# Holding the low part of q on all 128 rows in the attention heads of a two-layer trunk

## The chip, the cores and the metric

The kernel runs on one core of one Trainium2 chip, as a single launch. The metric is the device time of that launch in microseconds, the median of several runs. The profile is of one execution and gives for each instruction its engine, its start and its duration. TensorE is called PE, its weight loads PEld, VectorE DVE, ScalarE ACT, GpSimd POOL and SyncE SP.

## What is computed

Two layers work on x of 256 tokens by 1024 features in float32. Each layer is a half-weight SwiGLU network, a mixer and a second SwiGLU network, each followed by a residual sum and a layer norm. Both mixers hold attention heads of width 64: layer 0 has 12 heads whose softmax is masked by a dilated pattern, layer 1 has 8 heads of stick-breaking attention beside 4 mLSTM heads of width 128. For a head, what matters here is only the product of q and k ahead of the softmax:

```python
scores = jnp.einsum("bdhnqe,bdhnke->bdhnqk", qb, kb).astype(jnp.float32) / math.sqrt(dh)   # layer 0
z = jnp.einsum("bhqd,bhkd->bhqk", qblk, kt).astype(jnp.float32) / math.sqrt(dh)            # layer 1
```

## The kernel before

**Split products.** Products run in the type float32r. Every operand is split into a high part, rounded to that type, and a low part, what is left; a product of two matrices is then high x high, high x low and low x high. Weights stream in 166 chunks of 1 MB (class `Weights`): SP loads a chunk into a raw buffer, ACT makes the high part (L83), DVE the low part (L84), in four pieces per chunk. The layer's activations lie transposed in `xh` and `xl`, and a projection (`mmB`, L211 to L218) runs, for half a chunk, 8 k-tiles x 3 products of 256 columns.

**The mixers.** `mixer0` (L559) and `mixer1` (L631) project q and k in groups of four heads: `proj_qk` (L550) takes two chunks, one with the q and one with the k of two pairs of heads. There are five groups, three in layer 0 and two in layer 1. A projection leaves two banks of 128 rows; rows 0 to 63 belong to the first head of a pair and rows 64 to 127 to the second. `HALF` names these two slices, `i` is the head in the pair and `j` the pair.

**The stacked layout.** Heads are 64 wide, the array has 128 rows. `stack_q` writes the high part of q on both halves of the rows for each head (`qq`, four copies on ACT, L460) and the low part only on the head's own half (`ql`, DVE, L462). `stack_k` writes the high part of k on the head's own half and its low part on the other half (`kk`, ACT L468, DVE L470). So one product of 128 rows, `qq` x `kk` (L477), sums high x high and high x low, and a second product of 64 rows, `ql` x the high half of `kk` (L478), adds low x high. `scores64` does this for two token tiles, so a head has four products on PE, taken in turn from L477 and L478.

**The order around them.** `steps()` is called after each half chunk of a projection and runs, for head k, the scores and the softmax (s1), for head k-2 the product with v (s3, L514, whose results take 64 columns of the array) and for head k-1 the transposes of its weights (s2, L483 on PE, then the copy L486 on ACT). The softmax is L581 to L588 in layer 0 and L703 to L714 in layer 1, on DVE and ACT. Its small memsets (L709, L710) run on POOL, as do the `pow` of every layer norm (L291) and a mask that layer 1's mixer builds (L638). The Tile framework plans the order of each engine's queue at compile time, by its own model of times, with data dependencies and buffer releases as its limits; `hp()` moves a block forward in it.

**Buffers.** `qq`, `ql` and `kk` come from the pool `gp`, tag "g": 11 slots, each of the size of the largest tile of the tag, 4 KB per row. The hidden tiles of the SwiGLU networks use the same slots.

Of the kernel before, what the change touches and what calls it, by code (L numbers as in the profile page):

```python
# [11 lines left out]
F32 = mybir.dt.float32  # L12
# [5 lines left out]
P = 128  # L18
# [10 lines left out]


class Weights:
    """Streams the weight matrices through SBUF in chunks of [128, 2048]: each
    is loaded once and split exactly into hi + lo, both float32r."""

    def __init__(self, nc, raw_pool, w_pool, chunks):
        self.nc, self.raw_pool, self.w_pool, self.chunks = nc, raw_pool, w_pool, chunks
# [9 lines left out]
        self.next = 0  # L46

    def load_part(self, j0, j1):
        """The first chunk, by quarters."""
        (ap,), k, c = self.chunks[0]  # L50
        if j0 == 0:
            self.raw[0] = self.raw_pool.tile([P, k * c], F32, tag="raw", name="raw0")
        rv = self.raw[0].rearrange("p (k c) -> p k c", k=k)
        for j in range(j0, j1):
            self.nc.sync.dma_start(rv[:, 2 * j:2 * j + 2, :], ap[:, 2 * j:2 * j + 2, :])
        self.loaded = 1
# [62 lines left out]
def kernel(ctx: ExitStack, tc: tile.TileContext, a, cmask, out):  # L119
# [34 lines left out]
    def MM():  # L154
        return ps_mm.tile([P, 512], F32, tag="mm", name=nm("mm"))

# [1 line left out]
    def cols(w, c0):  # L158
        return ([a[w][:, c0:c0 + 256].rearrange("(k p) c -> p k c", p=P)], 8, 256)

# [20 lines left out]
    chunks += ffn_chunks("l1_ffn2")  # L181
    W = Weights(nc, raw_pool, w_pool, chunks)

# [1 line left out]
    X = [const.tile([P, D], F32, name=f"X{t}") for t in range(2)]  # L185
    for h in range(2):
        for t in range(2):
# [19 lines left out]
        bcast(gb[:, 0, :], pre + "_g", D, nc.sync)  # L207
        bcast(gb[:, 1, :], pre + "_b", D, nc.sync)

# [1 line left out]
    def mmB(i, j, bank, off):  # L211
        hi, lo = W.get(i)
        cs = slice(j * P, (j + 1) * P)
# [44 lines left out]
        nc.scalar.copy(hi, src)  # L258
        nc.vector.tensor_tensor(lo, src, hi.bitcast(F32), OP.subtract)

# [1 line left out]
    def transpose_x(t, halves=(0, 1), scale=True):  # L262
        for hf in halves:
            b = MM()
# [32 lines left out]
                    nc.sync.dma_start(out[0, t * P:(t + 1) * P, hs], X[t][:, hs])  # L297

    def ln_last(t, accs):
        """The closing norm, by column groups in the order in which they end."""  # L300
        st = sm(24, "stl")
        mv = sm(4, "mvl")
        for c, w in COLS3:
            nc.vector.tensor_tensor(X[t][:, c:c + w], accs[c][:, 0:w], X[t][:, c:c + w], OP.add)
            for q in range(c // 256, (c + w) // 256):
                nc.vector.bn_stats(st[:, q * 6:q * 6 + 6], X[t][:, q * 256:(q + 1) * 256])
        nc.vector.bn_aggr(mv[:, 0:2], st)
        nc.vector.tensor_scalar(mv[:, 2:3], mv[:, 1:2], EPS, None, op0=OP.add)
        nc.gpsimd.tensor_tensor(mv[:, 3:4], mv[:, 2:3], mhalf[:, 0:1], OP.pow)
        for h in range(2):  # L310
            hs = slice(h * 512, (h + 1) * 512)
            nc.vector.scalar_tensor_tensor(Y[:, hs], X[t][:, hs], mv[:, 0:1], gb[:, 0, hs], OP.subtract, OP.mult)
        for q in range(4):
            qs = slice(q * 256, (q + 1) * 256)
            nc.vector.scalar_tensor_tensor(X[t][:, qs], Y[:, qs], mv[:, 3:4], gb[:, 1, qs], OP.mult, OP.add)
            (nc.sync, nc.scalar)[q % 2].dma_start(out[0, t * P:(t + 1) * P, qs], X[t][:, qs])

    def out_proj(ys, nxt, last=False, hooks=()):
        """Rows of ys (slots of two k-tiles) times the next chunks, residual and
        norm; the token tiles run one after the other over the last chunks, so  # L320
        that one's norm hides under the other's products. nxt: the stage that
        follows; hooks: run ahead of the first token tile's last chunks."""
        n = len(ys)
        ids = W.take(n)
        hooks = list(hooks)
        accs = [{c: ACC() for c, _ in COLS}, {}]
        cols = [COLS, COLS3 if last else COLS]

        def open_t1():
            for c, _ in cols[1]:  # L330
                accs[1][c] = MM() if c == 768 else ACC()

        if n > 4:
            open_t1()
        for c in range(n - 4):
            for t in range(2):
                mmO(ids[c], ys[c], t, accs[t], c == 0, False, cols[t])
                if t == 1:
                    W.free(ids[c])
                W.pump()  # L340
        for c in range(n - 4, n):
            h = hooks.pop(0) if hooks else None
            if h:
                h()
            mmO(ids[c], ys[c], 0, accs[0], c == 0, c == n - 1)
            W.pump()
        if n == 4:
            open_t1()
        ln_a(0, accs[0], last)
        if last:  # L350
            for g in COLS3:
                for c in range(n - 4, n):
                    mmO(ids[c], ys[c], 1, accs[1], False, c == n - 1, [g])
            ln_last(1, accs[1])
            return
        for c in range(n - 4, n):
            if c == n - 1:
                transpose_x(0)
            mmO(ids[c], ys[c], 1, accs[1], c == 0, c == n - 1)
            W.free(ids[c])  # L360
            W.pump()
        ln_a(1, accs[1])
        nxt()

    def stagger(n, per, done):
        """n chunks by token tiles, per of them to a bank: done(t, b, bank)."""
        ids = W.take(n)
        banks = {}
        for t in range(2):
            for c in range(n):  # L370
                if t == 0 and c == n - 1:
                    transpose_x(1)
                if c % per == 0:
                    banks[t] = MM()
                mmA(ids[c], t, banks[t], (c % per) * 256)
                if t == 1:
                    W.free(ids[c])
                W.pump()
                if c % per == per - 1:
                    done(t, c // per, banks[t])  # L380

# [1 line left out]
    def swiglu(bank):  # L383
        sg = T(256)
        nc.scalar.activation(sg, bank[:, 0:256], AF.Silu)  # L385
# [55 lines left out]
                split(y[:, j, 0, :], y[:, j, 1, :], g)  # L441
        out_proj(ys, nxt, last)

# [1 line left out]
    # scores of a head: [t1 s0 | t1 s1 | t0 s0], by (token tile, column, width)  # L445
    BLK = ((1, 0, 2 * P), (0, 2 * P, P))

    def scores(bank, q, k):
# [3 lines left out]
    HALF = (slice(0, 64), slice(64, 128))  # L452

    def stack_q(b, qq, ql):
        """q of two pairs of heads: hi over both halves of the rows for each
        head of a pair, lo where it stands."""
        v = b.rearrange("p (j t) -> p j t", j=2)
        for i, r in enumerate(HALF):
            for o in HALF[i:] + HALF[:i]:
                nc.scalar.copy(qq[o, i], v[r])  # L460
        for i, r in enumerate(HALF):
            nc.vector.tensor_tensor(ql[r], v[r], qq[r, i].bitcast(F32), OP.subtract)  # L462

    def stack_k(b, kk):
        """k likewise: hi where it stands, lo on the other half of the rows."""
        v = b.rearrange("p (j t) -> p j t", j=2)
        for i, r in enumerate(HALF):
            nc.scalar.copy(kk[r, i], v[r])  # L468
        for i, r in enumerate(HALF):
            nc.vector.tensor_tensor(kk[HALF[1 - i], i], v[r], kk[r, i].bitcast(F32), OP.subtract)  # L470

    def scores64(bank, qk, i, j):
        qq, ql, kk = qk
        r = HALF[i]
        for t, o, _ in BLK:
            ts = slice(t * P, (t + 1) * P)
            nc.tensor.matmul(bank[:, o:o + 256], qq[:, i, j, ts], kk[:, i, j, :], start=True, stop=False)  # L477
            nc.tensor.matmul(bank[:, o:o + 256], ql[r, j, ts], kk[r, i, j, :], start=False, stop=True)  # L478

    def transpose_p(p):  # L480
        b = MM()
# [41 lines left out]
    pair = []  # L523

    def slots():
        """y slots of two k-tiles, taken as they are first written."""
        got = {}

        def get(i):
            if i not in got:  # L530
                got[i] = GR()
            return got[i]

        return get

    def projB(dst, off, steps):
        """Two feature tiles of the next chunk into dst columns off.. (fp32)."""
        (i,) = W.take(1)
        b = MM()
        for j in range(2):  # L540
# [8 lines left out]

    def proj_qk(lst, steps):  # L550
        qq = g_pool.tile([P, 2, 2, S], F32R, tag="g", name=nm("qq"))
        ql = g_pool.tile([P, 2, S], F32R, tag="g", name=nm("ql"))
        stack_q(projB(None, 0, steps), qq, ql)
        kk = g_pool.tile([P, 2, 2, S], F32R, tag="g", name=nm("kk"))
        stack_k(projB(None, 0, steps), kk)
        lst.append((qq, ql, kk))

# [1 line left out]
    def mixer0():  # L559
        cw = sm(6, "cw")  # L560
        for c in range(2):
# [65 lines left out]
        assert step[0] == 12  # L627
        return [(yts, i) for i in (1, 2, 0, 3)], [steps, steps, conv_out]

# [1 line left out]
    def mixer1():  # L631
        gbias = sm(8, "gbias")
        bcast(gbias[:, 0:4], "l1_mlstm_b_i", 4)
        bcast(gbias[:, 4:8], "l1_mlstm_b_f", 4)
        bcast(msk[:, 384:896], "l1_mlstm_norm_g", 512)
        # strictly causal mask over [t1 s0 | t1 s1 | t0 s0]
        m3 = msk[:, 0:384]
        nc.gpsimd.memset(m3, 0.0)  # L638
        for o in (128, 256):
# [56 lines left out]
            nc.vector.tensor_copy(Bc, b[:, 0:8])  # L696
            nc.vector.tensor_tensor(ccv, gv[:, :, 0:4], Bc.rearrange("p (t c) -> p t c", t=2), OP.subtract)

        # stick-breaking heads
        def soft_sb(b):  # L700
            with hp():
                z = T()
# [14 lines left out]
        qs, qm = [], []  # L717
        sb = [att_head(qs, lambda t: vs[:, t * 512:(t + 1) * 512], h, yts, 4, soft_sb) for h in range(8)]

        # mLSTM heads  # L720
        nmu = sm(8, "nmu")
        den = sm(8, "den")
        num = []
# [72 lines left out]
        qkproj(qm)  # L796
        so = G()
        ids = W.take(2)
        # so: by pair of heads, token tile and head
        def final(g):  # L800
            def pv(tl):
                return tl.rearrange("p (t h) -> p t h", t=2)[:, :, 2 * g:2 * g + 2]
# [53 lines left out]
        final(1)  # L856
        return [(yts, i) for i in (2, 3, 0, 1)], [None, lambda: final_tr(0), None, lambda: final_tr(1)]

# [1 line left out]
    def start(banks):  # L860
        with tc.manual_schedule():
            for h in range(2):
# [35 lines left out]


def _pattern_mask():  # L900
    """8 ln(number of dilation patterns that pair t with s) over the blocks
    [t1 s0 | t1 s1 | t0 s0]; a shape-only constant."""
    i = np.arange(P)
    m = np.full((P, 3, P), 8 * NEG, np.float32)
    for b, (t0, s0) in enumerate(((P, 0), (P, P), (0, 0))):
# [26 lines left out]
```

## Time and profile before

| what | value |
|---|---|
| median of 3 runs | 1016.66 us (1014.95 to 1017.03) |
| span of the profiled execution | 1014.5 us |
| PE busy | 998.9 us (98%) |
| PE weight loads busy | 934.1 us (92%) |
| DVE busy | 617.7 us (61%) |
| ACT busy | 538.0 us (53%) |
| POOL busy | 20.9 us (2%) |
| read from HBM | 181.90 MB, 180 GB/s over the span |

The heads of layer 0 run from 236.8 to about 290 us, those of layer 1 from 729.6 to about 765 us. Busy times overlap between engines. The records of PE overlap too, because a matmul's end lies well behind the start of the next, so steps from start to start tell more of PE's pace than durations do.

### The profile page before, as it was taken

What the parts mean: (1) busy time and instruction counts of PE and PEld (TensorE: products, weight loads), DVE (VectorE), ACT (ScalarE), POOL (GpSimd) and SP (SyncE); (2) the same over time, 40 slices, a digit from 0 to 9 for tenths busy, and PEclk for the clock granted to TensorE, in tenths of its full rate; (3) what the DMA queues carried; (4) which work ended last, traced back from release to release, by engine and by line L of the source; (5) the groups of instructions that cost most, each with busy time, mean ns of one, the idle gap of its engine ahead of it and who ended that gap; (6) DMA issues with size and microseconds to landing.
All of it is one profiled execution on the core that took longest, in us unless ns stands there. A gap on an engine that the chain in (4) does not pass through costs nothing.

```text
span 1014.5 us, 17718 instructions
## 1 busy us (share of the span) xinstructions
PE 998.9 (98%) x7204; PEld 934.1 (92%) x7204; DVE 617.7 (61%) x1238; ACT 538.0 (53%) x1096; POOL 20.9 (2%) x54
## 2 busy tenths in 40 slices
PE   7999999999999999999999999999999999999997
PEld 6999998899879999998899999889989899999986
DVE  4765554667658756554675556447786786656434
ACT  4755453558646645443455555436776476545430
POOL 2000000000000000000000000000000100000000
PEclk9999999999999999999999999999999999999999
DMA  9876555474325755555476555646734367555511
GB/s 293 280 240 202 173 201 188 144 249 153 127 95 184 233 183 192 181 193 198 134 241 203 180 195 180 197 136 208 235 103 144 102 208 232 185 191 183 186 64 41
DMA packets 137314, 184.09 MB, mean 181 GB/s; under 512 B 4256, under 2 KB 121504, under 8 KB 137232
## 3 DMA queue, kind: packets, MB, share of 16 engines
q1 hardware_dynamic: 136672, 182.24, 54.5%
q8 instruction: 56, 0.92, 0.4%
q0 software_dynamic: 272, 0.47, 0.2%
q10 hardware_dynamic: 288, 0.26, 0.1%
q14 instruction: 26, 0.21, 0.1%
HBM read 181.90 MB, written 1.05 MB: 180 GB/s over the span
## 4 chain that ended last, share of the span: by engine, by line
PE 95%; DMA 2%; DVE 2%; ACT 1%; issue 0%; SPq 0%; POOL 0%; DVEq 0%; ACTq 0%; POOLq 0%
PE mm L218 17%; PE mm L216 17%; PE mm L217 17%; PE acc L251 9%; PE acc L253 9%; PE acc L255 9%; PE mm L236 4%; PE mm L235 4%; PE mm L237 4%; DMA raw<-in_l_ffn_w_in_dram 2%; PE acc L478 1%; PE acc L477 1%; PE mm L483 1%; PE mm L267 1%; PE acc L514 1%; DVE lo L84 1%
## 5 line engine op out<-in xcount | busy, mean ns | idle before, releaser
L84 DVE TENSOR_TENSOR lo<-raw,hi 128x512 fp32r<-128x512 f32 (+1 forms) x664 | 425.6, 685 | 254.0 <-ACT hi L83 252.8
L83 ACT CAST hi<-raw 128x512 fp32r<-128x512 f32 (+1 forms) x664 | 373.4, 618 | 295.8 <-PE mm L217 161.0
L216 PE MATMUL mm<-xh,hi 128*128 128x256 f32 x1456 | 411.2, 282 | 0.0
L218 PE MATMUL mm<-xh,lo 128*128 128x256 f32 x1456 | 409.4, 281 | 0.2 <-DVE lo L84 0.2
L217 PE MATMUL mm<-xl,hi 128*128 128x256 f32 x1456 | 409.0, 281 | 0.0
L218 PEld LDWEIGHTS mm<-xh,lo 128*128 128x128 f32 x1456 | 274.3, 188 | 0.7 <-DVE lo L84 0.4
L216 PEld LDWEIGHTS mm<-xh,hi 128*128 128x128 f32 x1456 | 274.4, 188 | 0.4
L217 PEld LDWEIGHTS mm<-xl,hi 128*128 128x128 f32 x1456 | 274.4, 188 | 0.0
L251 PE MATMUL acc<-hi,gr 128*128 128x512 f32 (+1 forms) x416 | 128.7, 387 | 0.0
L253 PE MATMUL acc<-lo,gr 128*128 128x512 f32 (+1 forms) x416 | 127.2, 384 | 0.0
L255 PE MATMUL acc<-hi,gr 128*128 128x512 f32 (+1 forms) x416 | 127.1, 384 | 0.0
L235 PE MATMUL mm<-hi,xh 128*128 128x256 f32 (+1 forms) x352 | 99.3, 282 | 0.0
L236 PE MATMUL mm<-lo,xh 128*128 128x256 f32 (+1 forms) x352 | 98.4, 279 | 0.0
L237 PE MATMUL mm<-hi,xl 128*128 128x256 f32 (+1 forms) x352 | 98.3, 279 | 0.0
L253 PEld LDWEIGHTS acc<-lo,gr 128*128 128x128 f32 x416 | 77.2, 188 | 15.1
L255 PEld LDWEIGHTS acc<-hi,gr 128*128 128x128 f32 x416 | 77.2, 188 | 14.9
L251 PEld LDWEIGHTS acc<-hi,gr 128*128 128x128 f32 x416 | 76.0, 188 | 14.6 <-issue 0.6
L236 PEld LDWEIGHTS mm<-lo,xh 128*128 128x128 f32 x352 | 66.2, 188 | 0.2
L235 PEld LDWEIGHTS mm<-hi,xh 128*128 128x128 f32 x352 | 66.2, 188 | 0.2
L237 PEld LDWEIGHTS mm<-hi,xl 128*128 128x128 f32 x352 | 66.2, 188 | 0.0
L385 ACT ACTIVATE t<-mm 128x256 f32<-128x256 f32 x88 | 33.6, 382 | 35.8 <-PE mm L218 27.8
L387 DVE SCALAR_TENSOR_TENSOR t<-t,mm 128x256 f32<-128x256 f32 x88 | 36.7, 417 | 13.1 <-ACT t L385 12.7
(163 smaller groups left out, 572.7 us busy)
## 6 DMA issues: line engine op xcount, KB each, us to landing
raw<-in_l_ffn_w_in_dram SPq DMA_DIRECT2D x87, 1024.0 KB, 5.1
raw<-in_l_ffn_w_out_dram SPq DMA_DIRECT2D x44, 1024.0 KB, 5.0
raw<-in_l_mix_w_in_dram SPq DMA_DIRECT2D x26, 1024.0 KB, 5.4
raw<-in_l_mix_w_out_dram SPq DMA_DIRECT2D x8, 1024.0 KB, 4.9
gb<-in_l_ln_g_dram SPq DMA_DIRECT2D x6, 512.0 KB, 5.4
gb<-in_l_ln_b_dram SPq DMA_DIRECT2D x6, 512.0 KB, 4.6
X<-in_x_dram SPq DMA_DIRECT2D x4, 256.0 KB, 4.9
raw<-in_l_ffn_w_in_dram SPq DMA_DIRECT2D x4, 256.0 KB, 8.5
```

The lines of the kernel that those rows point to most:

```text
L83: self.nc.scalar.copy(hi[:, sl], r[:, sl])
L84: self.nc.vector.tensor_tensor(lo[:, sl], r[:, sl], hi[:, sl].bitcast(F32), OP.subtract)
L216: nc.tensor.matmul(o, hi[:, kt, cs], xh[:, kt, :], start=kt == 0, stop=False)
L217: nc.tensor.matmul(o, hi[:, kt, cs], xl[:, kt, :], start=False, stop=False)
L218: nc.tensor.matmul(o, lo[:, kt, cs], xh[:, kt, :], start=False, stop=kt == 7)
L235: nc.tensor.matmul(o, xh[:, kt, ts], hi[:, kt, :], start=kt == 0, stop=False)
L236: nc.tensor.matmul(o, xh[:, kt, ts], lo[:, kt, :], start=False, stop=False)
L237: nc.tensor.matmul(o, xl[:, kt, ts], hi[:, kt, :], start=False, stop=kt == 7)
L251: nc.tensor.matmul(accs[c][:, 0:w], yh, hi[:, k, c:c + w], start=st, stop=False)
L253: nc.tensor.matmul(accs[c][:, 0:w], yh, lo[:, k, c:c + w], start=False, stop=False)
L255: nc.tensor.matmul(accs[c][:, 0:w], yl, hi[:, k, c:c + w], start=False, stop=sp)
L387: nc.vector.scalar_tensor_tensor(g, sg, 0.5, bank[:, 256:512], OP.mult, OP.mult)
```

## The change

`ql` gets a second index, the head in the pair, as `qq` has it, and is 128 rows for each head: the head's own half holds the low part of q and the other half zero. POOL writes the zeros, two memsets of 64 rows by 512 elements for each group. DVE writes the low parts as before, to their new place. In `scores64` the second product takes all 128 rows of `ql` and of `kk`; the rows of `kk` that hold the low part of k meet zeros. Comments and docstrings are dropped beside this, which does not alter the program.

```diff
@@ stack_q
         v = b.rearrange("p (j t) -> p j t", j=2)
+        for i, r in enumerate(HALF):
+            nc.gpsimd.memset(ql[HALF[1 - i], i].bitcast(F32), 0.0)
         for i, r in enumerate(HALF):
             for o in HALF[i:] + HALF[:i]:
                 nc.scalar.copy(qq[o, i], v[r])
         for i, r in enumerate(HALF):
-            nc.vector.tensor_tensor(ql[r], v[r], qq[r, i].bitcast(F32), OP.subtract)
+            nc.vector.tensor_tensor(ql[r, i], v[r], qq[r, i].bitcast(F32), OP.subtract)
@@ scores64
         qq, ql, kk = qk
-        r = HALF[i]
         for t, o, _ in BLK:
             ts = slice(t * P, (t + 1) * P)
             nc.tensor.matmul(bank[:, o:o + 256], qq[:, i, j, ts], kk[:, i, j, :], start=True, stop=False)
-            nc.tensor.matmul(bank[:, o:o + 256], ql[r, j, ts], kk[r, i, j, :], start=False, stop=True)
+            nc.tensor.matmul(bank[:, o:o + 256], ql[:, i, j, ts], kk[:, i, j, :], start=False, stop=True)
@@ proj_qk
-        ql = g_pool.tile([P, 2, S], F32R, tag="g", name=nm("ql"))
+        ql = g_pool.tile([P, 2, 2, S], F32R, tag="g", name=nm("ql"))
```

## Rows read from the trace of the kernel before

**Rows 1.** Page, part 4: the chain that ended last, by engine
```profile
PE 95%; DMA 2%; DVE 2%; ACT 1%; issue 0%; SPq 0%; POOL 0%; DVEq 0%; ACTq 0%; POOLq 0%
```
**Rows 2.** Timeline of PE, 234.8 to 238.3: start us, duration us, engine, line, tiles, rows
```profile
234.89 0.28 PE L218 MATMUL mm<-xh,lo 128*128 128x256 f32 x1
...
236.67 0.28 PE L218 MATMUL mm<-xh,lo 128*128 128x256 f32 x1
236.79 0.28 PE L477 MATMUL acc<-kk,qq 128*128 128x256 f32 x1
237.00 0.38 PE L478 MATMUL acc<-kk,ql 64*128 64x256 f32 x1
237.31 0.38 PE L477 MATMUL acc<-kk,qq 128*128 128x256 f32 x1
...
238.16 0.28 PE L217 MATMUL mm<-xl,hi 128*128 128x256 f32 x1
```
**Rows 3.** Timeline of PE's weight loads, same stretch and columns
```profile
236.67 0.19 PEld L477 LDWEIGHTS acc<-kk,qq 128*128 128x128 f32 x1
...
237.31 0.19 PEld L477 LDWEIGHTS acc<-kk,qq 128*128 128x128 f32 x1
```
**Rows 4.** Timeline of PE where L514 follows scores, and a projection (x8: merged)
```profile
249.67 0.28 PE L477 MATMUL acc<-kk,qq 128*128 128x256 f32 x1
...
250.81 0.87 PE L514 MATMUL acc<-t,g 128*64 128x256 f32 x8
...
743.62 0.27 PE L218 MATMUL mm<-xh,lo 128*128 128x256 f32 x1
743.82 0.87 PE L514 MATMUL acc<-t,g 128*64 128x256 f32 x8
```
**Rows 5.** Timeline of PE where the transposes follow a projection
```profile
246.38 0.28 PE L218 MATMUL mm<-xh,lo 128*128 128x256 f32 x1
246.50 0.49 PE L483 MATMUL mm<-ident,t 128*128 128x128 f32 x3
```
**Rows 6.** Timeline of PE, two and three heads in a row: first product, then transposes
```profile
240.87 0.28 PE L477 MATMUL acc<-kk,qq 128*128 128x256 f32 x1
...
243.27 0.55 PE L483 MATMUL mm<-ident,t 128*128 128x128 f32 x3
...
733.69 0.28 PE L477 MATMUL acc<-kk,qq 128*128 128x256 f32 x1
...
737.35 0.55 PE L483 MATMUL mm<-ident,t 128*128 128x128 f32 x3
```
**Rows 7.** ACT's timeline, then the chain's last piece before 748.59, then PE's timeline
```profile
736.70 0.52 ACT L708 ACTIVATE t<-t 128x384 f32<-128x384 f32 x1
737.98 0.48 ACT L486 COPY t<-mm 128x384 f32<-128x384 f32 x1 [0.76 <-PE mm L483]
...
747.85 0.69 DVE kk L470
748.59 0.38 PE L477 MATMUL acc<-kk,qq 128*128 128x256 f32 x1 [0.46 <-DVE kk L470]
```
**Rows 8.** Timeline of POOL (two memsets), then of DVE in layer 1
```profile
289.89 0.56 POOL L638 MEMSET msk<- 128x384 f32 x1 [83.59 <-DVE sc L581]
...
744.83 0.10 POOL L709 MEMSET t<- 128x3 f32 x1 [3.45 <-PE acc L514]
...
739.11 0.68 DVE L462 TENSOR_TENSOR ql<-mm,qq 64x512 fp32r<-64x512 f32 x1 [1.06 <-ACT qq L460]
```
**Rows 9.** PE's timeline at the start; busy by engine, clock, DMA at the end
```profile
11.79 0.41 PE L228 MATMUL mm<-xh,lo 128*128 128x256 f32 x1
12.01 0.41 PE L226 MATMUL mm<-xh,hi 128*128 128x256 f32 x1
...
1008.00:1014.50 6.50, 0.00 (x0) 0.00 (x0) 3.61 (x9) 0.00 (x0) 0.99 (x1) 0.76 0.24 81
```
**Rows 10.** What PE's queue runs for L477 beside products: duration ns min/median/max, starts
```profile
L477 PEldq EVENT_SEMAPHORE  x5: 51/51/51, 238.8 to 750.8; - x5
```

## The prediction

> **What bounds the kernel now.** I read the chain of waits first, then the timeline of TensorE (PE) through the attention heads, then that of the engines which feed it. The chain is 95% PE [rows 1], so a microsecond taken from PE's stream is a microsecond of the kernel unless another chain takes over at that place. In the stream of the projections a product starts every 0.118 us: 15 steps between 234.89 and 236.67 [rows 2]. A weight load starts one product ahead: the load for the first score product starts at 236.67, when the last projection product starts, and that score product starts at 236.79 [rows 2, 3].
>
> At the scores this rhythm breaks. A head has four products, two of L477 (128 rows) and two of L478 (64 rows), taken in turn. The first L478 starts 0.21 us after L477, the next L477 0.31 us after that, and its weight load now starts together with it, at 237.31, not a product ahead [rows 2, 3]. From the head's first product to the second one after its last there are 5 steps and 1.37 us (236.79 to 238.16), where five steps of the stream are 0.59. All products here have 256 columns and the weight loads take 0.19 us on either kind, so the length of the work does not explain it. What differs is the number of rows from one product to the next. I read the excess as a price for each change between 64 and 128 rows: PE runs empty and the load can't go ahead. The change removes all of these except where another form follows.
>
> **The change, part by part.**
>
> *Score products (the gain).* 20 heads, 40 products of L478. Their first operand becomes 128 rows; columns, count and bank stay. A product then has the form of the projections, so I price it at 0.118 from [rows 2]. The bounds are 0.118 and the present 0.31; I take the first, because L477 itself, 128 rows with the same right-hand tile, starts 0.12 after a projection product [rows 2]. By what follows the scores on PE:
> - a projection follows (4 heads, starting at 236.79, 255.41, 274.53, 729.61; the first stands in [rows 2]): 1.37 - 5 x 0.118 = 0.78 each, 3.12 us.
> - the product with v, L514, follows (7 heads; one stands in [rows 4], 249.67 to 250.81): 1.14 now. L514 uses 64 columns of the array, another form, and costs 0.20 to enter from a stream of 128 rows (743.62 to 743.82, [rows 4]). After: 3 x 0.118 + 0.20 = 0.55. Gain 0.59 each, 4.1 us.
> - the transposes L483 follow (4 heads on their own): they enter from a stream at 0.12, like any product (246.38 to 246.50, [rows 5]). The head's four products take the same 1.14 as above: 1.14 - 4 x 0.118 = 0.67 each, 2.7 us.
> - two heads in a row, then L483: 240.87 to 243.27, 2.40 - 8 x 0.118 = 1.46 us [rows 6].
> - three heads in a row, then L483: 733.69 to 737.35, 3.66 - 12 x 0.118 = 2.24 us [rows 6].
>
> Sum on PE alone: 3.12 + 4.1 + 2.7 + 1.46 + 2.24 = 13.6 us. The transposes themselves I leave as they are.
>
> *What is late next.* In layer 0 PE waits for nothing during its heads. In layer 1 it waits 0.46 us at 748.59 for kk, before the first head of the second group [rows 7]. The chain of waits shows what stands before that: from 737.98 to 747.85 and its end it runs through ACT and DVE alone, from the copy L486 to the lo part of k, L470 [rows 7]. That chain starts from the transposes at 737.35, behind the three heads in a row. ACT sat idle 0.76 us before L486 [rows 7]; before that it ends the sigmoid of 736.70 at 737.22, and that work hangs on the projection of q and not on the scores. So however early PE gets there, the chain moves by 0.76 and not by 2.24, and the wait at 748.59 grows from 0.46 to some 1.9 us. Loss: 2.24 - 0.76 = 1.5 us. For the other heads I count no loss: between a head's scores and its transpose there are at least 24 projection products, and both ends move together.
>
> *Memsets (added).* Two for each of five groups, 64 x 512 fp32 on POOL. The nearest row is the 128x384 memset, 0.56 us [rows 8]; by elements 0.75 each, 1.5 per group. The bounds are 0.56, the row itself, and twice my value; POOL is idle nearly all the time, so neither end reaches the sum. POOL is in order but runs ahead of the program: L638, a memset of layer 1's mixer, stood in its queue at 289.89 with 83.59 us of waiting behind it [rows 8]. So the memset should start when its slot of the g pool comes free. For the last group of layer 0 I take that to be the end of head 3's scores (249.67 plus 1.14, [rows 4]), with L462 13 us later. If that cover were gone, L462 would wait on DVE and everything behind it there, the next lo parts and the softmax; that is priced below as a rival.
>
> *The lo part of q (L462).* Same two instructions per group, same 64 x 512; only the place written differs. Nothing. ql grows from 2 to 4 KB per row, but its slot has the size of the largest tile of its tag, which qq and kk already fill, so no slot is lost.
>
> *A new wait on PE.* L478 now also depends on POOL. L477 shows five such extra waits of 0.051 us, one per group [rows 10]. As many again: 0.26 us; bounds 0 and 0.5.
>
> *A rule against it.* [Rows 2, 3] show a load starting while a product on the same 128 rows runs. The Trainium skill, "TensorE: Matmul & The Clock Gate", section "Part 3: Packing small matmuls — row/col tiling", says that a weight load overlaps running matmuls only when their row groups differ. By that rule putting all score products on the same rows would win nothing. The trace of the projections disagrees with it; the case stands below as the third rival.
>
> **Sum.** 13.6 - 1.5 - 0.26 = 11.8 us. The profiled execution has a span of 1014.5 us, the median of the runs is 1016.66, 2.2 us more; what lies around the span is not touched. 1016.66 - 11.8 = 1004.8 us (span 1002.7).
>
> **The rivals.**
> 1. *ACT and DVE take more of it.* If what happens after the three heads holds for every place where the transposes follow, two thirds (1.5 of 2.24) of 2.7 + 1.46 are lost as well, 2.8 us: 1007.6. For it: a head's transpose waits for its softmax. Against: PE doesn't wait once in layer 0's heads, so there is some slack.
> 2. *The memset is held in POOL's queue.* In layer 1 POOL also carries the small memsets of the heads, and one waits to 744.83 for a product [rows 8]. If ql's memsets of the second group stood behind that pair, they would end at about 744.83 + 0.26 + 1.5 = 746.6, and L462, first due at 739.11 [rows 8], would hold DVE for 7.5 us. Of that 1.5 lies in the wait that I already count: up to 6 us, 1010.8. Against: its slot comes free before any head begins.
> 3. *No change.* The price belongs to the tile pair q x k and not to the number of rows: the loads do not go ahead and steps stay at 0.31. Then only the new wait is left, 1016.9. Against: L218 to L477, both 128 rows, is 0.12 [rows 2].
> 4. *Slower: TensorE's clock.* At the end of the span, with no product in 6.5 us, the granted clock has a mean of 0.76, so it dropped from 2.4 to 1.2 GHz on the way [rows 9]. At the start, after a wait, products of 256 columns step at 0.22 (11.79 to 12.01, [rows 9]) instead of 0.118, 0.1 more. If the wait at 748.59 grew so much that the clock fell there, each product after it would cost that much; with 118 products at the slow step, five half chunks of 24 (8 k-tiles x 3), the 11.8 us are gone, and with seven half chunks the time is 1016.66 - 11.8 + 16.8 = 1021.7. Against: the wait that I work out is 1.9 us, and PE had waited 0.46 there without any effect.
>
> **How the numbers follow.** Forecast 0.75 (1004.8; from 1003.1 with no loss to 1006.6 with the losses twice as large); rival 1: 0.10; rival 2: 0.06; rival 3: 0.05; rival 4: 0.04. The range: at the low end the 1003.1 and 1.7 below it, since the lowest of the runs before lies 1.7 under their median: 1001.4. At the high end it takes in rival 1 with 1.4 us of the same spread: 1009.0. Left out are rivals 2 to 4, 0.15 together, and the edge of the forecast. A measurement of this kernel can tell a change of about 0.2%, 2 us. Faster: forecast and rivals 1 and 2, 0.91. Same: rival 3, 0.05. Slower: rival 4, 0.04.
>
> **What would show it.** In the changed kernel's timeline L477 and L478 start 0.118 apart with loads one product ahead, and L478's form reads 128 rows; a head before a projection takes 0.47 us, one before L514 0.55. PE's wait for kk, near 739 (748.6 less 8.1 us won in layer 0 and 1.5 behind it), is 1.5 to 2.3 us. POOL shows ten memsets of 0.5 to 1.5 us, each over before its L462 starts, and nobody waits for them. I am wrong in the sum if the steps of the scores stay above 0.15; in the losses if PE shows waits before L483, or if the wait for kk stays under 1 us; and altogether if the planner writes another order of the products.

## The result and the profile after

The changed kernel takes 1004.49 us (median of 4 runs, 1002.80 to 1004.63), the kernel before, run beside it, 1016.19 us (4 runs, 1014.95 to 1017.03): a ratio of 0.9884, with an interval from 0.9871 to 0.9897. The forecast was 1004.8. The profiled execution has a span of 1002.9 us where that of before has 1014.5.

In after.py the lines from L458 on have moved down by two and those from L477 on by one: L478 is qq x kk, L479 is ql x kk, L484 the transposes, L515 the product with v, L459 the new memset, L464 the lo part of q, L472 that of k, L487 the copy behind the transposes. First the page of the changed kernel, parts 1 and 4:

```profile
PE 986.2 (98%) x7204; PEld 929.9 (93%) x7204; DVE 617.9 (62%) x1238; ACT 537.3 (54%) x1096; POOL 26.1 (3%) x64
...
PE 93%; DMA 3%; DVE 2%; ACT 1%; issue 0%; SPq 0%; POOL 0%; DVEq 0%; POOLq 0%; ACTq 0%
```

PE has as many products as before and is busy 12.7 us less; POOL is busy 5.2 us more, with ten instructions more. PE still carries the chain, 93% of it where it was 95% [rows 1]; two more executions of the changed kernel (e5 and e7 below) show 94%.

Next, PE's timeline where [rows 2, 3] showed the first head (columns as there):

```profile
236.78 0.28 PE L218 MATMUL mm<-xh,lo 128*128 128x256 f32 x1
236.90 0.28 PE L478 MATMUL acc<-kk,qq 128*128 128x256 f32 x1
237.02 0.28 PE L479 MATMUL acc<-kk,ql 128*128 128x256 f32 x1
237.14 0.28 PE L478 MATMUL acc<-kk,qq 128*128 128x256 f32 x1
237.26 0.28 PE L479 MATMUL acc<-kk,ql 128*128 128x256 f32 x1
237.38 0.28 PE L216 MATMUL mm<-xh,hi 128*128 128x256 f32 x1
```

The timeline of the weight loads in the same stretch:

```profile
236.79 0.19 PEld L478 LDWEIGHTS acc<-kk,qq 128*128 128x128 f32 x1
236.91 0.19 PEld L479 LDWEIGHTS acc<-kk,ql 128*128 128x128 f32 x1
```

The head is no longer to be told from the projection around it: each product starts 0.12 us after the last, and each load starts with the product before its own. From the first score product to the first projection product behind them there are 0.48 us; four steps of the projection ahead of it take 0.47 (236.31 to 236.78 in the same view).

The whole saving lies in two places. I cut each trace at the first score product of a layer and at the first product with v behind the layer's last scores, both read from PE's timeline (times in us, kernels of the experiments below included):

| kernel | start to first score | heads of layer 0 | between | heads of layer 1 | rest | span |
|---|---|---|---|---|---|---|
| before | 236.79 | 52.29 | 440.53 | 34.03 | 250.86 | 1014.5 |
| after | 236.90 | 44.75 | 440.54 | 29.92 | 250.79 | 1002.9 |
| e1_order | 236.79 | 48.77 | 440.79 | 31.83 | 250.82 | 1009.0 |
| e2_zeros_only | 236.23 | 52.30 | 440.57 | 34.05 | 250.85 | 1014.0 |
| e3_no_lo | 235.91 | 42.82 | 440.56 | 27.98 | 250.83 | 998.1 |
| e4_pool_lo | 235.84 | 44.76 | 440.61 | 30.23 | 250.86 | 1002.3 |
| e5_after_again | 236.44 | 44.75 | 440.89 | 29.90 | 250.82 | 1002.8 |
| e6_lo_later | 236.45 | 44.76 | 440.83 | 28.61 | 250.85 | 1001.5 |
| e7_after_beside | 236.00 | 44.75 | 440.57 | 29.90 | 250.78 | 1002.0 |

Layer 0 gives 7.54 us and layer 1 4.11, together 11.65; the three other columns do not move with the change. The columns of the heads repeat to 0.02 us from one execution of a kernel to another (after, e5 and e7), while the start differs by up to 0.9 us between executions of the same kernel (236.00 to 236.90). So a few tenths in the heads are read from these columns, not from the times.

In the view of waits, two waits of PE's products lie in the heads after the change: 1.45 us for kk, which were 0.46 in before [rows 7], and 0.36 us for the softmax ahead of transposes, which are new. (Shorter waits of its weight loads come with the steps of the forecast below.) Both belong to one place in layer 1, the three heads in a row. PE's timeline there, to be held against [rows 6, 7]; what a product waited for stands in brackets:

```profile
725.51 0.28 PE L478 MATMUL acc<-kk,qq 128*128 128x256 f32 x1
...
726.82 0.28 PE L479 MATMUL acc<-kk,ql 128*128 128x256 f32 x1
727.46 0.52 PE L484 MATMUL mm<-ident,t 128*128 128x128 f32 x3 [0.36 <-DVE t L715]
...
739.67 0.38 PE L478 MATMUL acc<-kk,qq 128*128 128x256 f32 x1 [1.45 <-DVE kk L472]
```

The twelve score products start within 1.31 us; PE then waits for the softmax ahead of the transposes and, ten microseconds later, for kk. The chain of waits shows why (its pieces: start, length, what):

```profile
728.51 0.53 ACT t L709
...
729.06 0.48 ACT t L487
...
738.94 0.70 DVE kk L472
```

From L487 at 729.06 to the end of kk (738.94 + 0.70) there are 10.58 us, and in before, from the copy at 737.98 to the end of kk (747.85 + 0.69, [rows 7]), 10.56. This piece of ACT and DVE did not get shorter. What got shorter is the stretch ahead of it: from the first of the twelve products to the copy there were 4.29 us (733.69 to 737.98, [rows 6, 7]) and now there are 3.55, so 0.74 less; L487 now starts 0.02 behind L709, and the idle 0.76 is gone.

POOL's timeline shows the memsets:

```profile
205.47 0.93 POOL L291 TENSOR_TENSOR st<-st,mhalf 128x1 f32<-128x1 f32 x1 [13.65 <-DVE st L290]
206.46 3.40 POOL L459 MEMSET ql<- 64x512 f32 x6
...
691.22 2.25 POOL L459 MEMSET ql<- 64x512 f32 x4
```

Six for layer 0 in one go, 30 us ahead of its heads, and four for layer 1, also 30 us ahead.

### The profile page after: what moved, and what is told of

The parts are those of the page before. It is cut to its first block, busy times and chain, and to the rows that moved or that the text cites. A ratio compares the mean times of both kernels' runs of the same rounds, so it can differ in the third digit from the quotient of the medians.

```text
span 1002.9 us, 17735 instructions
## 1 busy us (share of the span) xinstructions
PE 986.2 (98%) x7204; PEld 929.9 (93%) x7204; DVE 617.9 (62%) x1238; ACT 537.3 (54%) x1096; POOL 26.1 (3%) x64
## 4 chain that ended last, share of the span: by engine, by line
PE 93%; DMA 3%; DVE 2%; ACT 1%; issue 0%; SPq 0%; POOL 0%; DVEq 0%; POOLq 0%; ACTq 0%
PE mm L218 16%; PE mm L216 16%; PE mm L217 16%; PE acc L251 9%; PE acc L253 9%; PE acc L255 9%; PE mm L236 4%; PE mm L235 4%; PE mm L237 4%; DMA raw<-in_l_ffn_w_in_dram 3%; PE mm L267 1%; PE mm L484 1%; PE acc L515 1%; DVE lo L84 1%; ACT hi L83 0%; PE acc L478 0%
## 5 line engine op out<-in xcount | busy, mean ns | idle before, releaser
L84 DVE TENSOR_TENSOR lo<-raw,hi 128x512 fp32r<-128x512 f32 (+1 forms) x664 | 425.9, 686 | 253.3 <-ACT hi L83 252.0
L387 DVE SCALAR_TENSOR_TENSOR t<-t,mm 128x256 f32<-128x256 f32 x88 | 36.8, 418 | 13.1 <-ACT t L385 12.7
```

What stands on the lines that cost most here:

```text
L84: self.nc.vector.tensor_tensor(lo[:, sl], r[:, sl], hi[:, sl].bitcast(F32), OP.subtract)
L387: nc.vector.scalar_tensor_tensor(g, sg, 0.5, bank[:, 256:512], OP.mult, OP.mult)
```

## The experiments

Theory A is the reading of the prediction: the price sits in each change of the number of rows from one product to the next. Rivals: the price belongs to the tiles or to the 64-row products themselves (B); the memsets or the greater ql move something; and, for the rest of the time, that DVE's other work stands behind the wait for kk, or that it does not.

**e1_order: the same products, fewer changes.** In the kernel before, a head's four products run in the order 128, 64, 64, 128 rows. Nothing becomes larger and nothing is dropped.

```diff
         for t, o, _ in BLK:
             ts = slice(t * P, (t + 1) * P)
-            nc.tensor.matmul(bank[:, o:o + 256], qq[:, i, j, ts], kk[:, i, j, :], start=True, stop=False)
-            nc.tensor.matmul(bank[:, o:o + 256], ql[r, j, ts], kk[r, i, j, :], start=False, stop=True)
+            st = t == 1
+            for full in (st, not st):
+                if full:
+                    nc.tensor.matmul(bank[:, o:o + 256], qq[:, i, j, ts], kk[:, i, j, :], start=st, stop=not st)
+                else:
+                    nc.tensor.matmul(bank[:, o:o + 256], ql[r, j, ts], kk[r, i, j, :], start=not st, stop=st)
```

> The kernel before, with the four products of a head in the order 128, 64, 64, 128 rows in place of 128, 64, 128, 64. Same products, same widths, the second token tile starts its bank region with the 64-row product. Theory A (a change between 64 and 128 rows is what costs): two changes per head in place of four; steps 0.21, 0.12, 0.31 and 0.22 to the next product, the second 64-row product about 0.12 to 0.17 after the first. Gain 0.39 for 4 heads before a projection, 0.19 for 7 before L514, 0.28 for 4 before the transposes, 0.7 and 1.1 for the two rows of heads, 5.8 us in all, some 0.5 lost at the wait for kk: about 1011 us. Theory B (a 64-row product is slow by itself, 0.31): the second 64-row product starts 0.31 after the first, 3.8 us less gain, about 1014.7 us.

Measured: 1010.15 us (1009.82 to 1010.71, 4 runs) against 1016.38 for before (13 runs), ratio 0.9937, interval 0.9923 to 0.9952. PE's timeline of the first head, whose qq x kk is L480 here and ql x kk L482:

```profile
236.79 0.28 PE L480 MATMUL acc<-kk,qq 128*128 128x256 f32 x1
237.00 0.50 PE L482 MATMUL acc<-kk,ql 64*128 64x256 f32 x2
237.43 0.39 PE L480 MATMUL acc<-kk,qq 128*128 128x256 f32 x1
...
237.76 0.28 PE L217 MATMUL mm<-xl,hi 128*128 128x256 f32 x1
```

Its weight loads (a row of x2 is two merged):

```profile
237.00 0.29 PEld L482 LDWEIGHTS acc<-kk,ql 64*128 64x128 f32 x2
```

The two 64-row products take 0.43 us from the first start to the 128-row product behind them, and their two loads, 0.18 each by the list of L482's instructions, fit into 0.29: the second load starts some 0.11 after the first, as in a stream. From the head's first product to the second projection product behind it there are 0.97 us, and in before there were 1.37 (236.79 to 238.16, [rows 2]). So 64-row products that stand together run at the stream's pace, and what costs is the change: A holds. That the tiles cost nothing is seen in the changed kernel, where qq and ql alternate as in before and step at 0.12: B falls with both of its halves. The saving of the whole kernel is 6.2 us by the medians and 5.7 in the two columns of the heads, half of what the change gives, for two reordered lines.

**e2_zeros_only: the greater ql and the memsets, products as before.**

```diff
     def scores64(bank, qk, i, j):
         qq, ql, kk = qk
+        r = HALF[i]
...
-            nc.tensor.matmul(bank[:, o:o + 256], ql[:, i, j, ts], kk[:, i, j, :], start=False, stop=True)
+            nc.tensor.matmul(bank[:, o:o + 256], ql[r, i, j, ts], kk[r, i, j, :], start=False, stop=True)
```

> The changed kernel with its larger ql and its ten memsets, but the second product takes the head's own 64 rows as before, so the zeros are written and never read. Theory A and memsets hidden: the time of the kernel before, 1016.2 us within 1.5. Memsets or the larger tile cost something (held in POOL's queue, or DVE's L464 waiting on them): 2 to 6 us more than before. If the memsets' wait helps by another planned order: less than before by over 1.5 us.

Measured: 1015.69 us (1015.16 to 1015.97, 10 runs) against 1016.38, ratio 0.9993, interval 0.9984 to 1.0002. POOL writes the zeros here as in the changed kernel (busy 26.1 us in both). The columns of the heads are those of before to 0.02 us. So the memsets and the larger ql cost nothing, and all of the saving belongs to the 128 rows of the product, the only thing in which this kernel differs from the changed one. This settles the second rival.

**e3_no_lo: the kernel before without the second product.** The low x high part of the scores is left out.

```diff
-            nc.tensor.matmul(bank[:, o:o + 256], qq[:, i, j, ts], kk[:, i, j, :], start=True, stop=False)
-            nc.tensor.matmul(bank[:, o:o + 256], ql[r, j, ts], kk[r, i, j, :], start=False, stop=True)
+            nc.tensor.matmul(bank[:, o:o + 256], qq[:, i, j, ts], kk[:, i, j, :], start=True, stop=True)
```

> The kernel before without its 64-row products: low x high of the scores is left out, 40 products of 128 rows remain for 20 heads. Theory A: no change of rows is left among the scores, so the time is that of the changed kernel less 40 x 0.118 = 4.7 us, of which the 6 products of three heads in layer 1 (0.7 us) win nothing because ACT and DVE set the next start there: about 1000.5 us. And from the first score of those three heads to the first score of the next group the time stays 14.1 to 14.2 us, as in the changed kernel, with PE waiting 2.4 us or so for kk. If the price lies in the heads and not in the change of rows: 1016.2 - 4.7 = 1011.5 us. If PE sets the next start in layer 1: 13.4 us from score to score and 999.8.

Measured: 1000.00 us (999.74 to 1000.58, 4 runs), ratio 0.9839, interval 0.9822 to 0.9855. In the columns of the heads it lies 3.87 us under the changed kernel (1.93 + 1.94). Forty products at 0.118 are 4.72. In layer 1 the 16 of them are 1.89, so nothing is missing there. In layer 0 the 24 are 2.83, and 0.90 is missing; most of it stands in one wait for the softmax, 0.8, that the changed kernel does not have. The waits of PE's products in the heads (total, times, longest; the line of L587 is that of layer 0):

```profile
PE acc L477 <- DVE kk L470: 0.9, 1, 0.9
PE mm L482 <- DVE t L587: 0.8, 1, 0.8
PE mm L482 <- DVE t L713: 0.7, 1, 0.7
```

So in the changed kernel the 40 products cost about their steps in the stream, as far as two kernels with different waits can show it. Before, they cost 15.5 us by the same columns (9.47 + 6.05), and 16.4 by the medians (1016.38 - 1000.00).

One expectation failed. From the first score product of the three heads to that of the next group I had expected some 14.1 us, as in the changed kernel (725.51 to 739.67, 14.16), and it was 13.11 (722.37 to 735.48). The chain there still runs through ACT and DVE alone, but the planner wrote another order for them: two copies of qq stand back to back at 722.57, and one piece of weights less stands ahead of kk's lo part. So the length of that chain hangs on the order that the planner chooses, and an experiment that drops products also changes that.

**e4_pool_lo: the weights' lo parts off DVE.** In the changed kernel, DVE splits pieces of weights between the softmax and kk's lo part (L84 at 736.68 and 737.62). Here POOL does that for the two chunks that fall there.

```diff
-        self.nc.vector.tensor_tensor(lo[:, sl], r[:, sl], hi[:, sl].bitcast(F32), OP.subtract)
+        eng = self.nc.gpsimd if i in (126, 127) else self.nc.vector
+        eng.tensor_tensor(lo[:, sl], r[:, sl], hi[:, sl].bitcast(F32), OP.subtract)
```

> The changed kernel, with the low parts of two weight chunks (126 and 127, eight pieces) made on POOL instead of DVE. In the changed kernel six of those pieces stand in DVE's queue between the three heads of layer 1 and the low part of k, and PE waits 1.7 us there. Theory A (ACT and DVE set that start): with the pieces gone the low part of k ends about 2 us earlier, the wait for kk falls below 0.4 us, and the time is 1.3 to 1.6 us below that of the changed kernel. Rival (the softmax or the copies of q set it): the wait stays above 1.2 us and the time is the same. Second rival (POOL is slow and in order, a head's small memsets stand behind the pieces): the wait for kk falls, but DVE or PE waits for POOL at the next heads instead, and the time is the same or up to 3 us more.

Measured: 1004.62 us (1004.05 to 1004.70, 4 runs) against 1015.70 for before (7 runs), ratio 0.9888, interval 0.9873 to 0.9903. **e5_after_again** is the changed kernel on the same chip:

> The changed kernel once more, beside the run above on the same chip, as what that is compared with: 1004.5 us within 1.

1004.22 us (1003.63 to 1004.51, 4 runs), ratio 0.9884, interval 0.9867 to 0.9900. No gain, and the heads of layer 1 are 0.33 us longer. POOL's timeline:

```profile
733.56 8.47 POOL L85 TENSOR_TENSOR lo<-raw,hi 128x512 fp32r<-128x512 f32 x6
```

DVE's timeline, with the softmax in lines L714 (the scan) and L716:

```profile
733.64 2.04 DVE L714 TENSOR_TENSOR_SCAN t<-t,sep 128x386 f32<-128x386 f32 x1 [0.80 <-POOL t L712]
735.78 1.40 DVE L716 TENSOR_TENSOR t<-t,t 128x384 f32<-128x384 f32 x1
737.10 0.41 DVE L260 TENSOR_TENSOR gr<-acc,gr 128x256 fp32r<-128x256 f32 x1
...
742.27 0.96 DVE L714 TENSOR_TENSOR_SCAN t<-t,sep 128x386 f32<-128x386 f32 x1 [2.65 <-POOL t L712]
```

PE's timeline at kk:

```profile
738.28 0.38 PE L479 MATMUL acc<-kk,qq 128*128 128x256 f32 x1 [1.17 <-DVE kk L473]
```

The wait for kk fell from 1.45 to 1.17 only; the second rival of the expectation came. What DVE no longer had to do, it lost again in two ways. It waited for the small memsets of the softmax, now queued behind the pieces on POOL (0.80 us ahead of kk, 2.65 behind it). And its own instructions beside POOL's took up to two and a half times as long (L716 1.40 and, in the changed kernel, 0.55; the scan 2.04, and 0.96 where POOL had finished). The theory that less work on DVE shortens the wait is not refuted by this, since DVE did not get less to do in the end.

**e6_lo_later: the same work on DVE, later.** In the changed kernel, the projection of k of layer 1's second group no longer has pieces of weights split within it; they follow behind it, and their lo parts are issued only after kk's lo part. Helper lines are left out:

```diff
+        if self.after is not None:
+            with self.tc.issue_after(self.after):
+                self.nc.vector.tensor_tensor(lo[:, sl], r[:, sl], hi[:, sl].bitcast(F32), OP.subtract)
...
-        stack_k(projB(None, 0, steps), kk)
+        last = stack_k(projB(None, 0, steps, pump), kk)
+        if not pump:
+            W.after = last.ins
+            W.pump()
+            W.pump()
...
-        proj_qk(qs, steps)
+        proj_qk(qs, steps, False)
```

> The changed kernel, with the weight pieces that the projection of k in layer 1's second group would start traced behind the low part of k, and their DVE half queued behind it: the same work on the same engines, later. No weight piece is left in DVE's queue between the copies of q and the low part of k. Theory A (ACT and DVE set the start of the second group): the wait for kk falls from 1.5 us to under 0.4, and that for the first transpose stays at about 0.4 or falls; the time is 1.2 to 2 us below the changed kernel's: about 1002.7 us. Rival (the pieces are only moved: the wait comes back as a wait for weights or at the next heads): the wait for kk falls and another of over 1 us appears behind it on PE; the time is that of the changed kernel within 0.5.

Measured: 1003.10 us (1002.65 to 1003.24, 4 runs) against 1016.55 for before (7 runs), ratio 0.9864, interval 0.9847 to 0.9880. **e7_after_beside** is the changed kernel beside it:

> The changed kernel beside the run above on the same chip: 1004.4 us within 1, the wait for kk 1.5 us.

1003.69 us (1003.23 to 1003.87, 4 runs), ratio 0.9870, interval 0.9855 to 0.9885. PE's timeline in e6, whose transposes are L491 and whose qq x kk is L485:

```profile
737.86 0.27 PE L491 MATMUL mm<-ident,t 128*128 128x128 f32 x1
738.00 0.39 PE L485 MATMUL acc<-kk,qq 128*128 128x256 f32 x1
```

Its waits of PE, of which this line alone lies in the heads:

```profile
PE mm L491 <- DVE t L727: 0.6, 2, 0.4
```

The wait for kk is gone, and the heads of layer 1 are 1.29 us shorter than in e7 (28.61 and 29.90). A wait for the softmax ahead of two transposes grew, from 0.4 to 0.6. Here the planner also split the three heads in a row into two and one, so that not all of the 1.29 need come from DVE's order alone; the two were not told apart, and how much DVE's order alone is worth stays open. The span is only 0.5 shorter, because its start happened to be 0.45 later and the stretch between the layers 0.26 longer. The medians differ by 0.6 us, where 1.2 to 2 were expected, and the intervals of the two ratios overlap. It is the fastest version of these that keeps all of the scores, by a margin that the heads' column shows and the times hardly do.

## Why the prediction was right, by its steps

**The price per change (13.6 us).** Right. Steps of 0.118, loads a product ahead, as forecast; a head before a projection takes 0.48 (forecast 0.47), and one before L515 takes 0.56, of which 0.21 is the entry (forecast 0.55 and 0.20):

```profile
247.67 0.28 PE L478 MATMUL acc<-kk,qq 128*128 128x256 f32 x1
...
248.02 0.28 PE L479 MATMUL acc<-kk,ql 128*128 128x256 f32 x1
248.23 0.44 PE L515 MATMUL acc<-t,g 128*64 128x256 f32 x2
```

e1 showed the cause, with products of both kinds in another order. The Trainium skill, "TensorEngine Tiling (Array Packing)", section "Key Properties", says that changing the tiling mode drains the engine; the trace agrees with it, at 0.21 to 0.32 us a step where a stream has 0.12. The rule of the third rival does not hold here: loads of 0.19 us start with the product before their own though both use all rows.

**The loss in layer 1 (1.5 us).** Right in sum and mechanism: ACT and DVE give 0.74 of the 2.24 back (forecast 0.76), and the heads of layer 1 are 4.11 us shorter, where the terms of the forecast for these heads give 4.06, without that for semaphores. It is split otherwise than forecast: 0.36 of it is waited ahead of the first transposes and 1.45 for kk, not some 1.9 at kk alone. The wait at kk ends 0.05 below the 1.5 to 2.3 that the forecast named. The forecast had also named waits before the transposes as a sign that its losses are wrong, and that sign came: the sum of this loss holds, its place does not. In e6, where DVE's queue has another order, the wait for kk is gone.

**No loss elsewhere.** Wrong by 0.55 us. In layer 0 the terms add up to 8.09 and the trace gives 7.54. PE's timeline has the places, the entries to the transposes of two heads on their own and to the first scores of the second and the third group:

```profile
244.22 0.28 PE L218 MATMUL mm<-xh,lo 128*128 128x256 f32 x1
244.48 0.52 PE L484 MATMUL mm<-ident,t 128*128 128x128 f32 x3
...
252.14 0.28 PE L218 MATMUL mm<-xh,lo 128*128 128x256 f32 x1
252.38 0.55 PE L484 MATMUL mm<-ident,t 128*128 128x128 f32 x3
...
252.88 0.28 PE L217 MATMUL mm<-xl,hi 128*128 128x256 f32 x1
253.09 0.38 PE L478 MATMUL acc<-kk,qq 128*128 128x256 f32 x1
253.31 0.28 PE L479 MATMUL acc<-kk,ql 128*128 128x256 f32 x1
```

These steps are 0.26, 0.24, 0.21 and 0.22; in before the first three were 0.12 (the first stands in [rows 5]). With the third group, 0.14 and 0.22 (269.54, 269.68 and its next product), the excess over 0.12 a step is 0.14 + 0.12 + 0.19 + 0.12 = 0.57 us. The timelines show what these products waited for. DVE's after the change (L589, x2, is the end of a softmax):

```profile
243.79 0.55 DVE L589 TENSOR_SCALAR t<-t,sc 128x256 f32<-128x256 f32 x2
...
252.35 1.41 DVE L472 TENSOR_TENSOR kk<-mm,kk 64x512 fp32r<-64x512 f32 x2
```

The timeline of the weight loads after the change:

```profile
252.37 0.31 PEld L484 LDWEIGHTS mm<-ident,t 128*128 128x128 f32 x3 [0.16 <-DVE t L589]
...
253.09 0.19 PEld L478 LDWEIGHTS acc<-kk,qq 128*128 128x128 f32 x1
```

DVE's timeline in before (L588 is the same end of the softmax):

```profile
244.97 0.55 DVE L588 TENSOR_SCALAR t<-t,sc 128x256 f32<-128x256 f32 x2
```

The first transposes come right behind the end of their softmax (244.34), the second wait for theirs by name, and the load of L478 starts 0.05 behind the first of kk's two lo parts (0.69 each, so 253.04). For the first place, the end of the softmax lies 8.73 us behind the first score product in before (236.79 to 245.52) and 7.44 after (236.90 to 244.34): it moved by 1.29, while PE had won 0.78 + 1.46 = 2.24 by then. So the step that failed is that the two ends of a head, its scores and its transposes, "move together", with "PE waits for nothing during its heads" read as slack to spare: in before that softmax ended only 0.98 ahead of its transposes. Rival 1 had the mechanism, that ACT and DVE take a part, with a price five times too high.

**The new semaphore waits on PE (0.26 us).** Wrong, they do not exist. The lists of the instructions of L478 and L479 (duration in ns, least, median, most; first and last start):

```profile
L478 PEldq EVENT_SEMAPHORE  x5: 51/51/51, 238.1 to 741.2; - x5
...
L479 PEld LDWEIGHTS acc<-kk,ql x40: 187/189/192, 236.9 to 751.8; 128*128 128x128 f32 x40
L479 PE MATMUL acc<-kk,ql x40: 277/281/285, 237.0 to 751.9; 128*128 128x256 f32 x40
```

L478 has its five, as in [rows 10], and L479 none. So the sum charged 0.26 that does not exist and left out 0.55 that does; its gain is 0.2 too high by the trace (11.8 against 11.65), and 1004.8 stands nearer to 1004.49 than the terms deserve.

**The memsets.** Nothing waited for them, as forecast. Each takes 0.52 us, not 0.75, just under the lower bound of 0.56; and the memsets of layer 0's third group did not wait for head 3: all six ran at 206.46, right behind the layer norm. I had a wrong picture of which slot that group gets.

**The clock.** The fourth rival did not come. Two microseconds around the wait for kk, then six behind it: the granted clock (third number from the right) stays at 1.00, the 2.4 GHz level, with PE busy 0.55 of the two.

```profile
738.00:740.00 2.00, 0.55 (x4) 0.33 (x4) 1.94 (x4) 0.73 (x2) 0.00 (x0) 1.00 0.56 164
740.00:746.00 6.00, 6.00 (x53) 5.55 (x52) 5.73 (x10) 4.14 (x9) 0.40 (x4) 1.00 0.75 252
```

## What to carry to other kernels

A short product with half the rows among full ones costs far more than its own time: here 15.5 us for 40 products, against 3.9 by the same columns (4.7 by their steps) when they run on all rows, with zeros on the idle half. Read the starts, not the durations, on both sides of each change of form; where zeros can't be had, ordering the products so that equal forms stand together gives half of it. And before you count the whole gain, follow the chain of the engines that feed PE from one place of waiting to the next: what it can't give back, and every margin ahead of it that is smaller than the gain, comes off the sum.

## What the runs showed of the hardware beyond this

In e4, instructions of DVE with two inputs from SBUF took longer while POOL read SBUF. Beside POOL's subtractions (1.41 us for 128x512), the scan took 2.04 us instead of 0.96 and L716 took 1.40 instead of 0.55, while L260 and the lo part of kk, which read one of their inputs from PSUM, kept their 0.41 and 0.70 us. The Trainium skill, "SBUF — State Buffer", section "Who interferes with whom", says that a DVE instruction with two SBUF inputs contends with a GpSimd instruction that reads SBUF and not with one that only writes it. The trace agrees on both: beside the six memsets of the changed kernel (206.46 to 209.86), which only write, two of DVE's subtractions L84, both inputs in SBUF, took 1.28 us together, as two in a row also do with POOL idle (at 733.56), by its timeline:

```profile
207.77 1.28 DVE L84 TENSOR_TENSOR lo<-raw,hi 128x512 fp32r<-128x512 f32 x2
```
